# An FFN down projection whose Winograd sums are made earlier and kept in memory

## The chip, the cores and the metric

The kernel runs on one core of a Trainium2 chip. The core has a matmul engine (TensorE, PE in the profile, with its weight loads as PEld), three engines for elementwise work (VectorE or DVE, ScalarE or ACT, GpSimd or POOL), a queue engine that issues all transfers (SyncE or SP), 16 DMA engines, an on-chip memory of 128 partitions (SBUF) and accumulation banks of 128 x 512 float32 (PSUM). The metric is the device time of one execution in microseconds; lower is better. Before the change it is 1144.55 us, the median of three runs (1143.79 to 1145.27).

## What is computed

Two sequences of 512 tokens go through one encoder block, each with 16 shared meta tokens in front: norm, input projection, a gated depthwise convolution beside multi-head latent attention, output projection with residual, and a gated feed-forward network. Only the last part is touched:

```python
hf = _rms(h, ffn_norm_g[i])
h = h + (jax.nn.silu(hf @ w_gate[i]) * (hf @ w_up[i])) @ w_down[i]
...
return _rms(h, final_norm_g)[:, N_META:]
```

h has 1024 tokens by 1024 features, the hidden width D_FF is 2816, that is 22 blocks of 128. All is float32, and must come out at float32 accuracy.

## The kernel before

**Three matmuls for one.** PE multiplies in fp32r, a format with fewer mantissa bits. Each operand is split: ACT copies the rounded high part (L1094 in the down stage, L964 in gate and up), DVE or POOL subtracts it from the value to give the low part (L1096, L966). `mm3` (L151) then issues high·high, high·low and low·high (L158) into the same PSUM bank.

**Winograd's form of Strassen.** All three FFN products are done as 2 x 2 blocks with seven products instead of eight. With blocks a11, a12, a21, a22 of the left side and b11 to b22 of the right, the sums are s1 = a21 + a22, s2 = s1 − a11, s3 = a11 − a21, s4 = a12 − s2 and t1 = b12 − b11, t2 = b22 − t1, t3 = b22 − b12, t4 = b21 − t2 (t4 with that sign in this kernel).

**Gate and up.** 22 units, a gate unit and an up unit for each of the eleven pairs of hidden blocks. A unit has seven products of 12 matmuls of 128x512. While it runs, `comb` makes the operands of the next unit: DVE the sums (L948), ACT the high parts, POOL the low parts. `result` evacuates: DVE adds partial results, ACT applies silu in gate units, DVE multiplies in up units (L1000). The four blocks g of a pair (128 hidden features by 512 tokens each) are stored to memory in `g_dram` (L1001), 256 KB a store. The tiles that hold them (named slots and h) serve the next pair again.

**Down.** The first twenty hidden blocks make ten pairs, taken in three chunks of 3, 3 and 4 pairs. For a chunk, each of the seven products accumulates over the chunk's pairs in four banks: 12 matmuls of 128x512 for a product and a pair, a step. A pair's g and w_down blocks are loaded (L1074), `combine` makes their sums on DVE, in five operations of up to 128x1024 (L1080 to L1084), and `operands` makes the high and low parts for each product (L1094, L1096), the low part on DVE or, two times in seven, on POOL. After each chunk, every product's four banks are added into totals in SBUF (L1207 on ACT for some of the first chunk, L1209 on DVE); after the last chunk the totals are combined (L1178). The last two hidden blocks are multiplied in the ordinary way, eight products or 96 matmuls (operands named re), and with their results go the residual, the final norm and the output, tile by tile (L1231 to L1239).

**What sets the order.** The program text is not the order. A scheduler places each instruction on its engine's queue when it expects its inputs and buffers to be ready; on the chip each queue then runs strictly in that order, waiting where an input is late. SP too works in order: a store that waits for its data holds up the loads behind it.

Of the kernel before, what the change touches and what calls it, by code (L numbers as in the profile page):

```python
# [12 lines left out]
F32 = mybir.dt.float32  # L13
# [5 lines left out]
P = 128  # L19
D = 1024  # L20
# [53 lines left out]
LAST = 2  # L74
CHUNKS = (3, 3, 4)
DOWN_AHEAD = 3
DOWN_MOD = 7
DOWN_POOL = (1, 4)
LOAD_LEAD = (9, 10, 9)
FIRST_AT = {0: ((0, 0),), 1: ((0, 1), (1, 0)), 2: ((0, 2),), 3: ((0, 3), (1, 1),), 4: ((1, 2), (1, 3)), 5: ((2, 0), (2, 1)), 6: ((2, 2), (2, 3))}  # L80
POOL_SUMS = ()
LAST_AT = (1, 2, 3, 4)
LOAD_AT = 5
WO_AT = (4, 6)
FIN_POOL = 0
# [22 lines left out]
def encoder_kernel(ctx: ExitStack, tc: tile.TileContext, x, meta, gains, w_in, w_kr, small, conv_w, wq, wk, wv,  # L108
# [666 lines left out]
    g_dram = [dram.tile([P, NT], F32, name=f"g_dram{f}") for f in range(NFF)]  # L775
# [154 lines left out]
    class Unit:  # L930
# [61 lines left out]
        def result(self, s, e, bk, other, cs):  # L992
            sil = half(4 * s, e)[:, cs]
            if not self.up:
                nc.vector.tensor_add(sil, bk, parts[other][:, cs])
# [4 lines left out]
            nc.vector.tensor_mul(y, y, sil)  # L1000
            nc.sync.dma_start(g_dram[2 * self.p + e][:, s * SEQ:(s + 1) * SEQ], y)  # L1001

    units = [Unit(u) for u in range(NFF)]

# [40 lines left out]

    n_pairs = (NFF - LAST) // 2
    chunks = [list(range(sum(CHUNKS[:i]), sum(CHUNKS[:i + 1]))) for i in range(len(CHUNKS))]
    assert sum(CHUNKS) == n_pairs

    def flat(t):  # L1050
        return t.rearrange("p a b -> p (a b)")

    sets = [("act00_", ops), ("a12", comb), ("s2", comb), ("act01_", ops), ("s1", comb), ("act11_", ops)]

    def reuse(n, pool, x_):
        return flat(pool.tile([P, 4, SEQ], F32R, tag=f"{n}{x_}", bufs=1, name=name("re")))

    class Pair:

        def __init__(self, p):  # L1060
            self.p = p

        def load(self, part):
            if part == 0:
                self.x, self.y = (reuse(*sets[self.p % len(sets)], x_).bitcast(F32) for x_ in "hl")
            g0, g1 = g_dram[2 * self.p], g_dram[2 * self.p + 1]
            w0, w1 = w_down[2 * self.p], w_down[2 * self.p + 1]
            x_, y = self.x, self.y
            lo, hi = slice(0, 512), slice(512, 1024)
            for to, src in (((x_[:, 1024:1536], g0[:, lo]), (x_[:, 512:1024], w0[:, lo])),  # L1070
                            ((y[:, 1024:1536], g1[:, lo]), (y[:, 1536:], w1[:, lo])),
                            ((x_[:, 0:512], g0[:, hi]), (x_[:, 1536:], w0[:, hi]),
                             (y[:, 0:512], g1[:, hi]), (y[:, 512:1024], w1[:, hi])))[part]:
                nc.sync.dma_start(to, src)  # L1074

        def combine(self):

            x_, y = self.x, self.y
            tmp = self.tmp = stream.tile([P, 1024], F32, tag="raw", bufs=2, name=name("raw"))
            nc.vector.tensor_sub(x_[:, 0:1024], x_[:, 1024:], x_[:, 0:1024])  # L1080
            nc.vector.tensor_sub(tmp, y[:, 0:1024], x_[:, 0:1024])  # L1081
            nc.vector.tensor_add(x_[:, 1024:1536], x_[:, 1024:1536], tmp[:, 0:512])
            nc.vector.tensor_sub(x_[:, 1536:], y[:, 512:1024], x_[:, 1536:])
            nc.vector.tensor_sub(y[:, 1024:], y[:, 1024:], tmp)  # L1084

        def operands(self, j, n):

            def of(t, *at):
                return t.rearrange("p (k n) -> p k n", n=512)[:, at[0]:at[-1] + 1:at[-1] - at[0]]

            src = (of(self.x, 1, 2), of(self.y, 2, 3), of(self.tmp, 0, 1) if j == 2 else None, of(self.x, 0, 3),
                   of(self.x, 1, 2), of(self.y, 0, 3), of(self.y, 1, 2))[j]
            w = stream.tile([P, 2, 1024], F32R, tag="pair", bufs=4, name=name("wd"))
            nc.scalar.copy(w[:, :, 0:512], src)  # L1094
            eng = nc.gpsimd if n % DOWN_MOD in DOWN_POOL else nc.vector
            eng.tensor_sub(w[:, :, 512:], src, w[:, :, 0:512].bitcast(F32))  # L1096
            g = 1 if j in (0, 4, 6) else 0
            return w[:, g, :], w[:, 1 - g, :]

    pairs = [Pair(p) for p in range(n_pairs)]  # L1100
    steps = [(c, j, p) for c in range(len(chunks)) for j in range(7) for p in chunks[c]]
    made = {}

    loads = {}
    for n, (c, j, p) in enumerate(steps):
        if c and j < 2:
            free = steps.index((next(c for c in range(len(chunks)) if p - len(sets) in chunks[c]), 6, p - len(sets))) \
                if p >= len(sets) else 0
            for part in ((0,), (1, 2))[j]:
                loads.setdefault(max(n - LOAD_LEAD[part], free, 0), []).append((part, p))  # L1110

    def prepare(upto):
        while len(made) <= min(upto, len(steps) - 1):
            n = len(made)
            c, j, p = steps[n]
            made[n] = pairs[p].operands(j, n)
            at = chunks[c].index(p)
            if j == 1 and at < 2 or j == 2 and at + 2 < len(chunks[c]):
                pairs[chunks[c][at if j == 1 else at + 2]].combine()
            for part, p in loads.pop(n, ()):  # L1120
                pairs[p].load(part)


    def sum_tiles():
        s4_ = [reuse("s4", comb, x_).bitcast(F32) for x_ in "hl"]
        one = lambda t: [t[:, i * 1024:(i + 1) * 1024] for i in range(2)]
        return [hf2, [hres[2], hres[6]], one(s4_[0]), [hres[0], hres[4]], one(s4_[1]), [hres[1], hres[5]],
                [hres[3], hres[7]]]

    def load_h(j, s, e):  # L1130
        for t in range(4):
            nc.sync.dma_start(total[j][t // 2][:, t % 2 * 512:(t % 2 + 1) * 512],
                              h_dram[(4 * s + t) * 128:(4 * s + t + 1) * 128, e * 512:(e + 1) * 512])

    for u in units:
        nxt = units[u.u + 1] if u.u + 1 < NFF else None
        if u.u + 2 < NFF:
            units[u.u + 2].load()
        for j in range(7):
            u.product(j, slice(256, 512) if u.u == 0 else slice(0, 512))  # L1140
            if nxt:
                nxt.comb(j)
                continue
            for part, i in FIRST_AT.get(j, ()):
                if i < CHUNKS[0]:
                    pairs[i].load(part)
            if j >= 6 - DOWN_AHEAD:
                prepare(j - (6 - DOWN_AHEAD))
    total = sum_tiles()
    load_h(1, 0, 0)  # L1150
    load_h(3, 1, 1)
    load_h(5, 1, 0)
    load_h(6, 0, 1)
    for i in range(2):
        nc.gpsimd.tensor_sub(total[5][i], total[5][i], total[3][i])
    g_fin = gain(2)

    last_ops = []

    def load_last():  # L1160
        f = NFF - LAST + len(last_ops)
        if f >= NFF:
            return
        cells = [reuse(*sets[(n_pairs + len(last_ops)) % len(sets)], x_) for x_ in "hl"]
        res = []
        for cell, src in zip(cells, (g_dram[f], w_down[f])):
            raw = stream.tile([P, 1024], F32, tag="raw", bufs=2, name=name("raw"))
            nc.sync.dma_start(raw, src)
            hi, lo = cell[:, 0:1024], cell[:, 1024:]
            nc.scalar.copy(hi, raw)  # L1170
            for a in (slice(0, 512), slice(512, 1024)):
                nc.gpsimd.tensor_sub(lo[:, a], raw[:, a], hi[:, a].bitcast(F32))
            res.append((hi, lo))
        last_ops.append(res)

    def add_total(n, to, other, i):
        eng = nc.gpsimd if n in POOL_SUMS else nc.vector
        eng.tensor_add(total[to][i], total[to][i], total[other][i])  # L1178


    after = {1: ((0, 1, 0),), 2: ((1, 2, 0),), 3: ((2, 3, 2),), 4: ((3, 2, 4), (4, 4, 3)), 5: ((5, 5, 3),),
             6: ((6, 6, 2),)}

    for n, (c, j, p) in enumerate(steps):
        if p == chunks[c][0]:
            if (c * 7 + j) % 2:
                wide = [bank2() for _ in range(2)]
                outs = [wide[t // 2][:, t % 2, :] for t in range(4)]
            else:
                wide = None  # L1190
                outs = [bank() for _ in range(4)]
# [126 lines left out]
```

## Time and profile before

| | us |
|---|---|
| median of the runs | 1144.55 |
| profiled execution, device time | 1145.55 |
| its span, first to last instruction | 1143.8 |
| before the first product of gate and up in full width | 0 to 499 |
| gate and up | to 896.3 |
| down | 896.3 to the end |

The profile is of one execution. A row of a stage table gives its window, then for each engine the busy time and the instructions, then the granted clock of PE (1.00 is full speed), the share of time that the DMA engines were busy, and GB/s. A row of a group gives line, engine, operation, tiles written and read, shape, count, then busy time and mean ns of one, then the idle time of the engine right before these instructions and what ended it. A row in order of time gives start, duration, engine, line and what it was; in brackets the idle time ahead of it. A DMA row gives count, size and the median time from issue to landing. Matmuls overlap, so that the duration of one is longer than the distance to the next.

### The profile page before, as it was taken

How to read it: one execution, taken by the hardware profiler on the slowest of the kernel's cores; microseconds unless marked ns; L12 is line 12 of the kernel's file. 1: busy time of each engine (PE TensorE's matmuls, PEld its weight loads, DVE VectorE, ACT ScalarE, POOL GpSimd, SP SyncE). 2: the span in 40 equal slices, each digit the busy share in tenths (PEclk: the TensorE clock that was granted, in tenths of full speed). 3: DMA queues.
4: the chain of work that ended last, by engine and by line, in shares of the span. 5: the costliest groups of instructions: out<-in, count | busy, mean ns of one | idle time of the engine just before them, and what ended most of it. 6: DMA issues, size and time to landing. Idle time of an engine off the chain costs nothing.

```text
span 1143.8 us, 15672 instructions
## 1 busy us (share of the span) xinstructions
PE 1085.1 (95%) x5886; PEld 933.0 (82%) x5886; DVE 852.5 (75%) x1132; ACT 506.9 (44%) x858; POOL 555.8 (49%) x439
## 2 busy tenths in 40 slices
PE   4999998999989999899999999999999899899896
PEld 4999887888878999788888888888888688687775
DVE  5699997888887547995656565656563877979997
ACT  6455525787785535633322332232223344233425
POOL 6489735563562323584554455445543442223815
PEclk9999999999999999899999999999999999999899
DMA  8211111110111312322232223222313974110203
GB/s 279 78 38 39 45 41 55 37 56 1 38 38 59 127 38 93 136 86 77 90 93 73 77 89 94 73 77 89 95 53 112 357 258 138 37 37 1 74 1 147
DMA packets 38554, 98.01 MB, mean 86 GB/s; under 512 B 4544, under 2 KB 4800, under 8 KB 38480
## 3 DMA queue, kind: packets, MB, share of 16 engines
q1 hardware_dynamic: 38480, 97.02, 25.4%
q8 instruction: 46, 0.75, 0.3%
q14 instruction: 28, 0.23, 0.1%
HBM read 77.08 MB, written 19.92 MB: 85 GB/s over the span
## 4 chain that ended last, share of the span: by engine, by line
PE 64%; DVE 26%; POOL 3%; issue 3%; ACT 2%; DMA 2%; SPq 0%; POOLq 0%; DVEq 0%; ACTq 0%
PE pt L158 50%; PE ps L158 7%; DVE wd L1096 3%; DVE ps L336 3%; DVE ps L344 3%; PE pt L652 2%; PE pt L622 2%; DVE pacc L346 1%; POOL wd L1096 1%; DMA re<-in_w_down_dram 1%; DVE re L1178 1%; DVE raw L1081 1%; DVE slots L1209 1%; DVE hf L881 1%; DVE y L1237 1%
## 5 line engine op out<-in xcount | busy, mean ns | idle before, releaser
L158 PE MATMUL pt<-act_h,wc 128*128 128x512 f32 (+1 forms) x552 | 176.2, 382 | 0.1
L966 POOL TENSOR_TENSOR wc<-tt,wc 128x512 fp32r<-128x512 f32 x84 | 112.9, 1361 | 110.1 <-ACT wc L964 62.2
L158 PE MATMUL pt<-hn_h,wp 128*128 128x256 f32 (+2 forms) x576 | 131.9, 322 | 1.1 <-ACT hn_h L148 1.1
L158 PEld LDWEIGHTS pt<-act_h,wc 128*128 128x128 f32 x552 | 103.3, 190 | 19.9 <-issue 0.3
L158 PE MATMUL pt<-wd 128*128 128x512 f32 x444 | 107.1, 395 | 5.8 <-DVE wd L1096 4.8
L158 PE MATMUL ps<-wd 128*128 128x512 f32 x396 | 99.5, 407 | 10.0 <-POOL wd L1096 5.4
L158 PE MATMUL pt<-act_l,wc 128*128 128x512 f32 (+1 forms) x276 | 105.6, 383 | 3.5 <-DVE act_l L900 3.4
L964 ACT CAST wc<-tt 128x512 fp32r<-128x512 f32 x88 | 51.2, 617 | 122.8 <-PE pt L158 119.5
L158 PEld LDWEIGHTS pt<-wd 128*128 128x128 f32 x444 | 83.9, 190 | 25.9 <-DVE wd L1096 6.6
L158 PEld LDWEIGHTS pt<-hn_h,wp 128*128 128x128 f32 x576 | 96.5, 190 | 10.1 <-ACT hn_h L148 1.5
L158 PEld LDWEIGHTS ps<-wd 128*128 128x128 f32 x396 | 78.0, 198 | 28.8 <-POOL wd L1096 5.9
L1094 ACT CAST wd<-re 128x1024 fp32r<-128x1024 f32 x60 | 62.9, 1053 | 86.5 <-PE pt L158 36.1
L144 POOL TENSOR_TENSOR wp<-raw,wp 128x1024 fp32r<-128x1024 f32 x28 | 69.2, 2471 | 54.4 <-ACT wp L141 54.3
L1096 POOL TENSOR_TENSOR wd<-re,wd 128x1024 fp32r<-128x1024 f32 x16 | 49.8, 3114 | 93.6 <-ACT wd L1094 79.8
L158 PE MATMUL pt<-hn_l,wp 128*128 128x256 f32 (+2 forms) x288 | 93.2, 324 | 0.0
L1096 DVE TENSOR_TENSOR wd<-re,wd 128x1024 fp32r<-128x1024 f32 x44 | 65.3, 1493 | 21.0 <-ACT wd L1094 21.0
L597 POOL TENSOR_SCALAR p<-p,sst 128x512 f32<-128x512 f32 x64 | 44.1, 694 | 67.5 <-DVE sst L595 59.4
L158 PE MATMUL pt<-wp,act_h 128*128 128x256 f32 x384 | 71.4, 285 | 1.6 <-DVE h L844 1.5
L966 POOL TENSOR_TENSOR wc<-raw,wc 128x512 fp32r<-128x512 f32 x30 | 39.3, 1323 | 54.0 <-ACT wc L964 54.0
L158 PEld LDWEIGHTS pt<-act_l,wc 128*128 128x128 f32 x276 | 52.4, 190 | 13.6 <-DVE act_l L900 3.6
L158 PEld LDWEIGHTS pt<-wp,act_h 128*128 128x128 f32 x384 | 60.1, 192 | 2.0 <-DVE h L844 1.7
L314 POOL TENSOR_TENSOR pacc<-pacc,prod 128x512 f32<-128x512 f32 x43 | 58.3, 1356 | 7.0 <-ACT prod L312 4.3
(294 smaller groups left out, 2870.3 us busy)
## 6 DMA issues: line engine op xcount, KB each, us to landing
raw<-in_w_gate_dram SPq DMA_DIRECT2D x22, 512.0 KB, 3.8
g_dram<-slots SPq DMA_DIRECT2D x44, 256.0 KB, 2.2
re<-g_dram SPq DMA_DIRECT2D x40, 256.0 KB, 5.3
re<-in_w_down_dram SPq DMA_DIRECT2D x40, 256.0 KB, 5.3
raw<-in_w_in_dram SPq DMA_DIRECT2D x12, 512.0 KB, 3.7
slots<-in_w_up_dram SPq DMA_DIRECT2D x11, 512.0 KB, 3.5
h<-in_w_up_dram SPq DMA_DIRECT2D x11, 512.0 KB, 3.5
x<-in_x_dram SPq DMA_DIRECT2D x8, 512.0 KB, 4.8
```

Source lines behind the costliest of these rows:

```text
L144: nc.gpsimd.tensor_sub(lo[:, a], raw[:, a], hi[:, a].bitcast(F32))
L158: nc.tensor.matmul(out_ap, lhsT=w_, rhs=m_, start=first and i + j == 0, stop=last and i == n - 1 and j == 2)
L314: nc.gpsimd.tensor_add(acc, acc, to)
L336: nc.vector.scalar_tensor_tensor(a_, half_win(c, 0, i, HS + 1), k, a_, ALU.mult, ALU.add)
L344: nc.vector.scalar_tensor_tensor(m_, both[:, :, i:i + HS], k, m_, ALU.mult, ALU.add)
L597: nc.gpsimd.tensor_scalar(pr[:, real], pr[:, real], st[:, 2, t:t + 1], 1.0, op0=ALU.mult, op1=ALU.mult)
L622: nc.tensor.transpose(pt[:, t * 128:(t + 1) * 128], self.ps[t][:, n0:n0 + w], ident)
L652: nc.tensor.matmul(self.po, lhsT=v, rhs=p_, start=self.done + j == 1, stop=self.done + j == 5)
L964: nc.scalar.copy(w[:, 0:512], src)
L966: lo_eng.tensor_sub(w[:, 512:1024], src, w[:, 0:512].bitcast(F32))
L1094: nc.scalar.copy(w[:, :, 0:512], src)
L1096: eng.tensor_sub(w[:, :, 512:], src, w[:, :, 0:512].bitcast(F32))
```

## The change

The sums of the down product are no longer made in the down stage. Those of g (four DVE operations of 128x512 for a pair, `g_sums`) are made in the up unit, right after the results, and stored with g: a11 with s1, a12 with a22, s3 with s2, and s4, which makes 1.8 MB for a pair where it was 1 MB. Those of w_down (`w_sums`) are made in the gate and up units as well, in halves of 256 columns, two groups for a pair: load two blocks' halves into the one buffer of the tag "gain" (tile wt), four DVE operations of 128x256, two stores. The down stage then has 77 steps, seven products of eleven pairs, without chunks and without the two blocks done in the ordinary way. Each step loads its two blocks of 128x512 (`load_step`, two transfers of 256 KB, issued 12 steps ahead in the text, into places that hold eight steps) and makes its operands (`prepare`, high on ACT, low on DVE, never on POOL; 14 places). A product takes all eleven pairs in one accumulation of four banks; the next product uses four others. The results go straight to where they belong (`evacuate`): into hres, which is loaded again with the residual, and into the four tiles x_. The last product is taken a token tile at a time, and the final norm of tiles 4 to 6 follows each; of the last tile, the half that is ready is squared and scaled by the gain ahead.

```diff
-LAST = 2
-CHUNKS = (3, 3, 4)
-DOWN_AHEAD = 3
-DOWN_MOD = 7
-DOWN_POOL = (1, 4)
...
+DOWN_AHEAD = 4
+LOAD_AHEAD = 8
+ORDER_DOWN = (0, 1, 2, 4, 3, 6, 5)
...
             nc.vector.tensor_mul(y, y, sil)
-            nc.sync.dma_start(g_dram[2 * self.p + e][:, s * SEQ:(s + 1) * SEQ], y)
...
+    def g_sums(p, j):
+        a11, a21, a12, a22 = half(3, 0), half(3, 1), half(7, 0), half(7, 1)
+        s3_, s2_, s4_ = hf2[0][:, 0:512], hf2[0][:, 512:], hf2[1][:, 0:512]
+        if j == 5:
+            nc.vector.tensor_sub(s3_, a11, a21)
+            nc.vector.tensor_add(a21, a21, a22)
+            nc.sync.dma_start(d_a11s1[p], hres[3])
+        elif j == 6:
+            nc.sync.dma_start(d_a12a22[p], hres[7])
+            nc.vector.tensor_sub(s2_, a21, a11)
+            nc.sync.dma_start(d_s3s2[p], hf2[0])
+        elif j == 7:
+            nc.vector.tensor_sub(s4_, a12, s2_)
+            nc.sync.dma_start(d_s4[p], s4_)
...
+    def w_sums(p, r, j):
+        cs = slice(r * 256, (r + 1) * 256)
+        def cut(t):
+            return t.rearrange("p (i c) -> p i c", i=2)[:, :, cs]
+        if j == 0:
+            w_tile[0] = const.tile([P, 4, 256], F32, tag="gain", bufs=1, name=name("wt"))
+            for i in range(2):
+                nc.sync.dma_start(w_tile[0][:, 2 * i:2 * i + 2], cut(w_down[2 * p + i]))
+        w = w_tile[0]
+        b11, b12, b21, b22 = (w[:, i] for i in range(4))
+        if j == 3:
+            nc.vector.tensor_sub(b11, b12, b11)
+        elif j == 4:
+            nc.vector.tensor_sub(b12, b22, b12)
+            nc.sync.dma_start(cut(d_t1t3[p]), w[:, 0:2])
+        elif j == 5:
+            nc.vector.tensor_sub(b22, b22, b11)
+        elif j == 6:
+            nc.vector.tensor_sub(b21, b21, b22)
+            nc.sync.dma_start(cut(d_t4t2[p]), w[:, 2:4])
...
+    steps = [(j, p) for j in ORDER_DOWN for p in range(n_pairs)]
...
+    ld_places = ["act00_h", "act00_l", "a12h", "a12l"]
+    op_places = [None] * 4 + [n + x_ for n in ("s2", "act01_", "s1", "act11_", "s4") for x_ in "hl"]
...
+            nc.sync.dma_start(t[:, 0, :], a)
+            nc.sync.dma_start(t[:, 1, :], b)
...
+            nc.scalar.copy(w[:, :, LO], blocks[n])
+            nc.vector.tensor_sub(w[:, :, HI], blocks[n], w[:, :, LO].bitcast(F32))
...
             u.product(j, slice(256, 512) if u.u == 0 else slice(0, 512))
+            if u.up:
+                g_sums(u.p, j)
+                w_sums(u.p, 0, j)
+            elif u.p:
+                if j == 0:
+                    g_sums(u.p - 1, 7)
+                w_sums(u.p - 1, 1, j)
...
+    def evacuate(j, t, src):
+        if j == 0:
+            nc.scalar.copy(x_[t], src)
+            add_sum(t, 0, src)
+        elif j == 1:
+            add_sum(t, 0, src)
+        elif j == 2:
+            nc.vector.tensor_add(x_[t], src, x_[t])
+        elif j == 4:
+            add_sum(t, 1, src)
+            add_sum(4 + t, 1, src)
+        elif j == 3:
+            add_sum(t, 1, x_[t])
+            nc.vector.tensor_add(x_[t], src, x_[t])
+        elif j == 6:
+            add_sum(t, 1, src)
+            for e in range(2):
+                add_sum(4 + t, e, x_[t])
...
+    for n, (j, p) in enumerate(steps):
+        load_step(n + DOWN_AHEAD + LOAD_AHEAD)
+        prepare(n + DOWN_AHEAD + (n_pairs if n >= 5 * n_pairs else 0))
...
+            step_mm(n, t, sums[t], p == 0, p == n_pairs - 1)
+            if p == n_pairs - 1:
+                evacuate(j, t, sums[t])
```

Where the scheduler put the new work shows in three places. The first is SP's queue in the middle of gate and up, a pair's worth: before, with the loads of the next units and four stores of g,

```order
L1001 DMA g_dram8_3992<-slots_67 128x512
L1001 DMA g_dram9_3993<-slots_67 128x512
L1001 DMA g_dram8_3992<-slots_67 128x512
L1001 DMA g_dram9_3993<-slots_67 128x512
L940 DMA raw_984_6799<-in_w_gate_dram 128x1024
```

and after, with w sums of pairs 8 and 9 (wt is the tile of a group, d_t1t3 and d_t4t2 the memory blocks, here with the pair's number behind):

```order
L1031 DMA wt_1127_8116<-in_w_down_dram 128x2x256 x2
L1038 DMA d_t1t38_4036<-wt_1127_8116 256x1x256
L1043 DMA d_t4t28_4047<-wt_1127_8116 256x1x256
L938 DMA slots_67<-in_w_up_dram 128x1024
L1031 DMA wt_1142_8255<-in_w_down_dram 128x2x256 x2
L1038 DMA d_t1t39_4037<-wt_1142_8255 256x1x256
L938 DMA raw_992_6940<-in_w_gate_dram 128x1024
L1043 DMA d_t4t29_4048<-wt_1142_8255 256x1x256
```

The load of a group stands right behind the stores of the group before it, which read the same buffer, and a weight load stands between. The text has one group for a unit; the queue has two, and the last of the 22 groups stands in unit 12.

The second is DVE where the last token tile is made into FFN operands and the first gate unit runs (act_l, s2l and the like are low parts that PE waits for; L907 to L912 here are L909 to L914 before). Before there was no wt row among these:

```order
L898 TENSOR_TENSOR a12l_4708<-slots_67,a12h_4707 128x4x128
L1035 TENSOR_TENSOR wt_845_5654<-wt_845_5654 128x256
L903 TENSOR_TENSOR slots_67<-slots_67,px_827_5475 128x512
L1037 TENSOR_TENSOR wt_845_5654<-wt_845_5654 128x256
L898 TENSOR_TENSOR act11_l_4058<-slots_67,act11_h_4057 128x4x128
L906 TENSOR_TENSOR slots_67<-slots_67 128x512
L1040 TENSOR_TENSOR wt_845_5654<-wt_845_5654 128x256
L912 TENSOR_TENSOR act01_l_4056<-slots_67,act01_h_4055 128x4x128
L907 TENSOR_TENSOR slots_67<-slots_67,px_827_5475 128x512
L909 TENSOR_TENSOR slots_67<-slots_67 128x512
L1042 TENSOR_TENSOR wt_845_5654<-wt_845_5654 128x256
L912 TENSOR_TENSOR s2l_4712<-slots_67,s2h_4711 128x4x128
```

Four w sums of the first group now stand among them, ahead of s2l.

The third is DVE at the end of the last unit, where the operands of the first down steps (L1130; wd_1184 and wd_1186 are those of steps 2 and 3, the re tiles those of steps 4 to 9) alternate with the unit's results (L983 to L998):

```order
L983 TENSOR_TENSOR slots_67<-pt_1179_8591,h1_4063 128x512
L997 TENSOR_TENSOR slots_67<-pt_1179_8591,slots_67 128x512
L1130 TENSOR_TENSOR re_1201_8748<-re_1189_8681,re_1201_8748 128x2x512
L1130 TENSOR_TENSOR wd_1184_8637<-re_1183_8634,wd_1184_8637 128x2x512
L998 TENSOR_TENSOR slots_67<-slots_67 128x512
L1130 TENSOR_TENSOR re_1204_8783<-re_1190_8686,re_1204_8783 128x2x512
L997 TENSOR_TENSOR slots_67<-pt_1182_8615,slots_67 128x512
L1130 TENSOR_TENSOR re_1202_8765<-re_1189_8681,re_1202_8765 128x2x512
L1130 TENSOR_TENSOR re_1205_8800<-re_1190_8686,re_1205_8800 128x2x512
L997 TENSOR_TENSOR slots_67<-pt_1185_8640,slots_67 128x512
L998 TENSOR_TENSOR slots_67<-slots_67 128x512
L1130 TENSOR_TENSOR wd_1186_8662<-re_1183_8634,wd_1186_8662 128x2x512
```

Step 3's operand comes after those of steps 4 to 9; PE's queue has the first three steps in front of it, in the same order as its text.

More of the change, by code (lines that the diff above doesn't have):

```diff
@@ L1043, in encoder_kernel @@
     units[1].load()
[L1046 to L1110, printed above, removed]
+    n_pairs = NFF // 2
@@ L1143, in encoder_kernel @@
                 continue
[L1144 to L1155, printed above, removed]
-    g_fin = gain(2)
[L1158 to L1174, printed above, removed]
```

171 lines of the change are left out of this document (91 added, 80 removed).

## The prediction

> **What bounds the kernel now.** I read the page's busy times first, then busy time by stage, then PE's groups and PE in order of time in the last stage, and last the chain of waits there.
>
> ```profile
> span 1143.8 us, 15672 instructions
> PE 1085.1 (95%) x5886; PEld 933.0 (82%) x5886; DVE 852.5 (75%) x1132; ACT 506.9 (44%) x858; POOL 555.8 (49%) x439
> ```
>
> PE is busy 95%, but an average says little. By stage (columns: PE, PE's weight loads, DVE, ACT, POOL, granted clock, DMA share, GB/s):
>
> ```profile
> 480.00:500.00 20.00, 16.14 (x98) 14.81 (x99) 19.83 (x23) 9.88 (x20) 15.92 (x12) 0.84 0.27 83
> 500.00:880.00 380.00, 380.00 (x1678) 314.66 (x1677) 222.67 (x259) 112.48 (x200) 189.36 (x142) 1.00 0.26 82
> 880.00:896.00 16.00, 16.00 (x72) 13.26 (x71) 9.26 (x9) 3.49 (x4) 2.39 (x1) 1.00 0.90 301
> 896.30:1134.90 238.60, 222.81 (x937) 179.69 (x935) 212.39 (x194) 93.46 (x117) 94.75 (x42) 0.96 0.30 106
> ```
>
> From 500 to 896 (gate and up products) PE never stops, and DVE is busy 59%. From 896.3 to 1134.9 (down products) PE loses time, DVE is busy 89%, and the clock falls to 0.96. At 480 to 500, where gate products begin, DVE is full.
>
> ```profile
> L158 PE MATMUL pt<-wd 128*128 128x512 f32 x444 | 107.1, 395 | 5.8 <-DVE wd L1096 4.8 <-DVE hf L1209 0.7 <-ACT wd L1094 0.2
> L158 PE MATMUL ps<-wd 128*128 128x512 f32 x396 | 99.5, 407 | 10.0 <-POOL wd L1096 5.4 <-DVE wd L1096 3.8 <-ACT wd L1094 0.5
> L158 PE MATMUL pt<-re,re 128*128 128x512 f32 x96 | 21.9, 389 | 0.0
> ...
> 896.33 6.28 PE L158 MATMUL pt<-wd 128*128 128x512 f32 x27
> 902.45 0.61 PE L158 MATMUL ps<-wd 128*128 128x512 f32 x2
> ...
> 914.25 7.87 PE L158 MATMUL ps<-wd 128*128 128x512 f32 x22 [5.43 <-POOL wd L1096]
> 921.95 5.60 PE L158 MATMUL pt<-wd 128*128 128x512 f32 x24
> ...
> 1070.94 5.49 PE L158 MATMUL ps<-wd 128*128 128x512 f32 x12 [3.12 <-DVE wd L1096]
> ...
> 1112.96 21.92 PE L158 MATMUL pt<-re,re 128*128 128x512 f32 x96
> ```
>
> The down stage has 444 + 396 + 96 = 936 matmuls. Unhindered, 27 take 902.45 − 896.33 = 6.12 us, 0.2267 us each, so 936 need 212.2. The last ends at 1112.96 + 21.92 = 1134.9, 238.6 after the first: 26.4 too many. 15.8 of them are the waits in the groups' last column; the other 10.6 are slow matmuls right behind the waits (22 in 921.95 − 914.25 = 7.70 us, 0.35 each, where 0.2267 is the pace).
>
> **The rule and the row.** The Trainium skill, page "TensorE: Matmul & The Clock Gate", Part 1, says that PE's clock falls to half after an idle window of some 3.4 us and comes back after as long a busy one. By it only the 5.43 us wait costs anything behind itself. The trace disagrees: behind a wait of 3.12 us, a row of 12 matmuls still shows 5.49 us, about 0.45 each. I go by the trace, where a microsecond of waiting costs 26.4 / 15.8 = 1.67; by the rule the stalls of 3 us that I put in the sum below would stay 2.
>
> What PE waits for is always a finished operand (wd), and the chain of waits shows why one is late:
>
> ```profile
> 904.97 9.23 POOL L1096 TENSOR_TENSOR wd<-re,wd 128x1024 fp32r<-128x1024 f32 x1 [10.17 <-ACT wd L1094]
> ...
> 1064.21 2.23 DVE h L1178
> 1066.45 2.23 DVE slots L1178
> 1068.68 2.21 DVE wd L1096
> ```
>
> Either POOL's subtraction takes 9.23 us beside a busy DVE, or DVE does Winograd sums (L1080 to L1084), additions into the totals (L1209, L1178) and operands in turn, and the operand is last.
>
> **The change, part by part.** *Matmuls.* 77 steps of 12 make 924 in place of 936: 924 × 0.2267 = 209.5 us.
>
> *DVE in the down stage.* The sums of ten pairs go, and so does POOL's share of the operands. Left are 77 operands, 44 additions of 128x512 (per tile, seven products ask for 1, 1, 1, 2, 2, 3 and 1 of them) and the norms.
>
> ```profile
> L1096 DVE TENSOR_TENSOR wd<-re,wd x44: 1208/1218/3419, 885.7 to 1108.2; 128x1024 fp32r<-128x1024 f32 x44
> ...
> L1209 DVE TENSOR_TENSOR slots<-slots,pt 128x512 f32<-128x512 f32 x14 | 8.9, 678 | 1.1 <-PE pt L158 1.1
> ...
> L1094 ACT CAST wd<-re 128x1024 fp32r<-128x1024 f32 x58 | 60.8, 1053 | 77.1 <-PE pt L158 36.1 <-PE ps L158 34.8 <-DMA re<-in_w_down_dram 2.9
> ```
>
> 77 × 1.22 + 44 × 0.68 = 124 us, plus some 10 for the norms: 134 of 210, where 212 of 239 were busy. A step lasts PE 12 × 0.2267 = 2.72; its operand costs ACT 1.05 and DVE 1.22. Neither can hold PE up on the average, and no long DVE job is left to stand before an operand. Since an evacuation comes once in eleven steps into banks that the next product does not use, a wait for it goes too. I take all 26.4 us as removed inside the stage; the lower bound is that none is.
>
> *DMA in the down stage.* Each step loads 512 KB, so 524 KB / 2.72 us = 193 GB/s; 880 to 896 shows 301 GB/s carried. Loads are issued eight or more steps (21 us) ahead. Hidden.
>
> *The seam.* The order shows PE going from the last gate/up product to steps 0 to 2, whose operands ACT and DVE make while the last unit's results are still being evacuated, in buffers that its products free one by one. From the fourth product of that unit on (896.3 − 3 × 2.72 = 888.1) DVE has, by the order, 8 operands and 7 result operations up to step 3's operand: 8 × 1.22 + 7 × 0.68 = 14.5, so that is done near 903. PE has steps 0 to 2, 36 × 0.2267 = 8.2 us, and asks for it at 904.5. The margin of 2 us holds if every load is there in time. Best case no wait; worst, the 5.43 of today comes back, 9 with its slow matmuls. I take 3.
>
> *Added to gate and up.* Per pair, DVE gets four g sums of 128x512 and eight w sums of 128x256, and SP gets w loads and stores beside larger g stores. The order has the w sums of all pairs early: 22 groups, two in each unit, so within the first eleven of 22 units.
>
> ```profile
> L1000 DVE TENSOR_TENSOR slots<-slots 128x512 f32<-128x512 f32 x22 | 23.1, 1048 | 0.4
> L995 DVE TENSOR_TENSOR slots<-pt,slots 128x256 f32<-128x256 f32 x2 | 0.8, 420 | 0.1
> ...
> L948 DVE TENSOR_TENSOR tt<-raw,tt 128x512 f32<-128x512 f32 x20 | 34.8, 1742 | 25.0 <-POOL wc L966 25.0
> ...
> g_dram<-slots SPq DMA_DIRECT2D x40, 256.0 KB, 2.2
> ...
> h<-h_dram SPq DMA_DIRECT2D x2, 256.0 KB, 2.8
> ...
> re<-in_w_down_dram SPq DMA_DIRECT2D x40, 256.0 KB, 5.3
> ```
>
> Two units last 168 × 0.2267 = 38.1 us. DVE's 59% is 22.3 of them; 4 × 1.05 and 16 × 0.42 make 33.2. If each w sum also meets POOL as L1000 does (1.05 instead of 0.68), it is 39, just over. Behind a late DVE wait PE's results, and PE has three other banks: 3 × 12 × 0.2267 = 8.2 us of cover, gone only if the lateness adds up.
>
> It could add up, because the groups use one tile (wt) in turn: stores of one must land before the next is loaded, and DVE, which works in order, stands at the first sum until the load is there. A link: store 2.2, load 2.8, a second issue and two hand-overs about 0.4, so 5.4; its sums and what stands between them about 3. Four links in 38.1 us: 4 × 8.4 = 33.6. Hidden, with 4.5 to spare. Below: nothing. Above: a load of 5.3, as in the crowded down stage, makes a link of 10.9.
>
> At the stage's start, the order puts four w sums into the full 480 to 500 stretch, ahead of the operand s2l: 4 × 0.42 = 1.7, up to 7 if each meets POOL. I take 2 there and 2 for the rest: 4.
>
> *The end.* The last result then goes through one addition, half a square, the root and the scaling:
>
> ```profile
> 1135.27 0.68 DVE L1231 TENSOR_TENSOR slots<-pt,slots 128x512 f32<-128x512 f32 x1
> 1135.98 0.63 ACT L1232 ACTIVATE y<-slots 128x512 f32<-128x512 f32 x1 [1.08 <-DVE slots L1231]
> ...
> 1138.04 0.53 DVE L1233 SCALAR_TENSOR_TENSOR rs<-ms,ms 128x1 f32<-128x1 f32 x1 [0.61 <-ACT y L1232]
> 1138.64 0.55 POOL L1234 TENSOR_TENSOR rs<-rs,tiny 128x1 f32<-128x1 f32 x1
> ...
> 1139.23 0.75 DVE L1237 SCALAR_TENSOR_TENSOR y<-re,rs,gain 128x512 f32<-128x512 f32 x1 [0.66 <-POOL rs L1234]
> ```
>
> Now 1143.8 − 1134.9 = 8.9. Without the second half in between: 0.4 to the addition, 0.7, 0.8, 0.6, 0.6, 0.8, then 3.8 from 1139.98 to the end: 7.7.
>
> **Sum.** 896.3 + 4 + 209.5 + 3 + 7.7 = 1120.5 against 1143.8. That profiled run took 1145.55, 1.75 beside its span and 1.0 above the median of 1144.55; so 0.75 is added: **1121 us**, 2% less. This case's own range is 1113 (none of the two delays; 1114.3) to 1128.
>
> **Rivals.**
> *The seam stalls.* 9 us idle at the start of the stage, 15 with slow matmuls, for 3: 1133. For it: that is where today's longest wait stands. Against: no POOL, no sums there.
> *DVE is full in the first half of gate and up.* The Trainium skill, page "SBUF — State Buffer", "Who interferes with whom", has DVE and POOL share a port pair under an exclusive lock. The rows show it as L948's 1.74 us beside POOL. As a mechanism here: 16 w sums a pair at 0.42 + 1.0 make 22.3 + 4.2 + 22.7 = 49.2, but only about every other one meets POOL (busy 189 of 380): 41.2, 3.1 over, 5.5 times, 17 less the 8.2 of cover: 9, with slow clock 15: 1133.
> *The wt chain sets the pace: slower.* At links of 10.9, 43.6 per pair, 5.5 over, 5.5 times: 30, less 8.2: 22 idle, 22 to 37 lost where I put 2: 1141 to 1156, and I put it at 1150, the more as these stores and loads go in rows of 1 KB where the quoted ones have 2 KB or more. It costs from links of 9.5 on and turns the change slower at links between 10.6 (slow matmuls counted) and 11.1. For it: one buffer, in-order DVE and SP. Against: DMA share is 0.26 there, and a 256 KB load lands in 2.8.
> *The stalls stay.* If cast and subtraction alone made operands late, 26.4 return in place of 3: 1144. Against: 1.05 and 1.22 in 2.72.
>
> **Chances.** Forecast 0.69, seam 0.10, port 0.08, chain 0.09, stalls stay 0.04. Two tenths of a per cent (2.3 us) is about what a measurement can tell from none. Faster: 0.69 + 0.10 + 0.08 = 0.87; the same 0.04; slower 0.09. The range takes in the seam and port cases: 1113 to 1138.
>
> **What would show it.** PE's groups of the down stage: 924 matmuls, idle under 3 us, clock 1.00; the first of them between 896 and 901. DVE in that stage near 134. PE idle from 500 to 700 would speak for the chain (DVE then waits at L1035 for a DMA) or the port (DVE busy over 95%). Waits at steps 2 or 3 would speak for the seam. Wrong in the large: PE waiting for wd or re all through the stage, or for a load.

## The result, and the profile after

The changed kernel takes 1152.42 us, median of five runs (1150.46 to 1156.38). The kernel before, on the same chip, takes 1143.79. The ratio is 1.0081, with a 95% interval of 1.0058 to 1.0105: 0.8% slower, where I forecast 2% faster. The profiled execution is the slowest of the five, 1156.38 us. First the page, then busy time by stage (the columns are those of the prediction's table).

```profile
span 1154.6 us, 15888 instructions
PE 1089.3 (94%) x5874; PEld 935.1 (81%) x5874; DVE 837.4 (73%) x1197; ACT 499.0 (43%) x832; POOL 471.5 (41%) x409
```

```profile
480.00:500.00 20.00, 14.27 (x94) 13.24 (x95) 19.62 (x26) 10.77 (x21) 13.19 (x8) 0.83 0.41 132
500.00:720.00 220.00, 195.41 (x802) 155.97 (x801) 158.72 (x225) 52.68 (x96) 96.50 (x71) 0.95 0.54 175
720.00:937.90 217.90, 217.90 (x964) 180.46 (x963) 148.40 (x177) 69.90 (x118) 102.30 (x74) 1.00 0.40 133
937.90:1147.50 209.60, 209.60 (x925) 173.29 (x923) 125.88 (x131) 81.84 (x88) 8.70 (x14) 1.00 0.60 207
```

The down stage is what was hoped for: 209.6 us, PE never idle, clock 1.00. Before it took 238.6. But gate and up, which never stopped PE before, now lose 24.6 us of PE's time between 500 and 720, and the clock falls to 0.95 there. The two profiled executions' own times differ by 1156.38 − 1145.55 = 10.8 us, and three differences make that up:

| | before | after | difference |
|---|---|---|---|
| end of gate and up | 896.3 | 937.9 | +41.6 |
| down products | 238.6 | 209.6 | −29.0 |
| from the last matmul to the end | 8.9 | 7.1 | −1.8 |

In the view of waits, over the time from 478 on for PE and from 500 to 760 for DVE (columns: us in total, times, longest), the reason shows at once.

```profile
PE pt L151 <- DVE slots L997: 16.7, 9, 2.9
PE pt L151 <- DVE h L979: 6.7, 5, 2.7
```

```profile
DVE wt L1035 <- DMA wt<-in_w_down_dram: 44.0, 16, 6.0
...
DVE wt L1037 <- DMA wt<-in_w_down_dram: 4.3, 5, 1.4
```

PE waits for DVE to take its results out of the banks (L997, L979). DVE is not too busy for that (158.72 of 220 us): it stands at the first w sum of a group, L1035, for 44 us, because w_down's piece has not landed. In order of time, SP's and DVE's rows, a link of the chain through the one buffer wt looks like this.

```profile
565.44 0.56 SPq L1043 DMA_DIRECT2D d_t4t<-wt  x1
567.98 1.25 SPq L1031 DMA_DIRECT2D wt<-in_w_down_dram  x2
573.31 0.56 SPq L1038 DMA_DIRECT2D d_t1t<-wt  x1
575.78 0.56 SPq L1043 DMA_DIRECT2D d_t4t<-wt  x1
```

```profile
571.01 0.73 DVE L1035 TENSOR_TENSOR wt<-wt 128x256 f32<-128x256 f32 x1 [3.80 <-DMA wt<-in_w_down_dram]
571.67 0.68 DVE L983 TENSOR_TENSOR slots<-pt,h 128x512 f32<-128x512 f32 x1
572.27 0.67 DVE L997 TENSOR_TENSOR slots<-pt,slots 128x512 f32<-128x512 f32 x1
...
575.34 0.41 DVE L1042 TENSOR_TENSOR wt<-wt 128x256 f32<-128x256 f32 x1
```

At 565.44 the second store of a group is issued. It lands, and only then, at 567.98, can the loads into the same buffer go out; at 571.01 the first of the two loads has landed, which is all that the first sum reads, and DVE, which has stood still for 3.80 us, starts the four sums. Results that PE had ready meanwhile (L983, L997) come in between. The next second store goes out at 575.78: 10.3 us for this link. PE stands for 2.22 us behind that L997:

```profile
573.09 0.47 PE L151 MATMUL pt<-a12h,wc 128*128 128x512 f32 x1 [2.22 <-DVE slots L997]
```

The first and the last of 21 such stores between 500 and 740 are these.

```profile
508.18 0.56 SPq L1043 DMA_DIRECT2D d_t4t<-wt  x1
...
733.82 0.56 SPq L1043 DMA_DIRECT2D d_t4t<-wt  x1
```

(733.82 − 508.18) / 20 = 11.28 us a link. The rows between give the mean of its three parts: 3.10 from the store's issue to the load's, 3.47 from there to the first sum, 4.71 from the first sum to the next second store. A unit of gate and up lasts 19.04 us, and the order has two groups in each: 22.56 − 19.04 = 3.5 us too long, in ten or eleven units 35 to 39 us. What PE lost from 500 to 720 is 38.8: it did 802 matmuls there, and at full pace 973 (the row of before, quoted with the second experiment, has just that), so 171 × 0.2267. After 733.8, when the last group is done, PE never waits again.

### The profile page after: what moved, and what is told of

Same layout as the page of the kernel before. It is cut to its first block, busy times and chain, and to the rows that moved or that the text cites. A ratio compares the mean times of both kernels' runs of the same rounds, so it can differ in the third digit from the quotient of the medians.

```text
span 1154.6 us, 15888 instructions
## 1 busy us (share of the span) xinstructions
PE 1089.3 (94%) x5874; PEld 935.1 (81%) x5874; DVE 837.4 (73%) x1197; ACT 499.0 (43%) x832; POOL 471.5 (41%) x409
## 4 chain that ended last, share of the span: by engine, by line
PE 59%; DVE 21%; DMA 12%; issue 3%; ACT 2%; POOL 1%; SPq 1%; DVEq 0%; POOLq 0%; ACTq 0%
PE pt L151 41%; PE ps L151 12%; DMA wt<-in_w_down_dram 5%; DMA d_t4t<-wt 5%; DVE ps L329 3%; DVE ps L337 3%; PE pt L645 2%; PE pt L615 2%; DVE pacc L339 1%; DVE wt L1037 1%; DVE wt L1035 1%; DVE tt L946 1%; DVE wt L1042 1%; DVE hf L879 1%; DMA raw<-in_w_in_dram 1%
## 5 line engine op out<-in xcount | busy, mean ns | idle before, releaser
L176 POOL TENSOR_SCALAR ms<-ms 128x1 f32<-128x1 f32 (+1 forms) x24 | 12.8, 534 | 250.5 <-ACT re L175 213.8
L1130 DVE TENSOR_TENSOR re<-re,re 128x1024 fp32r<-128x1024 f32 x53 | 64.2, 1223 | 47.2 <-ACT re L1129 46.8
L1129 ACT CAST re<-re 128x1024 fp32r<-128x1024 f32 x53 | 55.2, 1054 | 68.0 <-PE ps L151 23.8
L151 PE MATMUL pt<-re 128*128 128x512 f32 x360 | 84.0, 389 | 0.0
L151 PEld LDWEIGHTS pt<-re 128*128 128x128 f32 x360 | 67.6, 188 | 14.0
L964 POOL TENSOR_TENSOR wc<-raw,wc 128x512 fp32r<-128x512 f32 x30 | 42.1, 1419 | 79.8 <-ACT wc L962 79.8
L151 PE MATMUL pt<-a12h,wc 128*128 128x512 f32 (+1 forms) x184 | 63.7, 411 | 10.7 <-DVE slots L997 10.6
L151 PE MATMUL pt<-s4h,wc 128*128 128x512 f32 (+1 forms) x184 | 60.1, 390 | 6.7 <-DVE h L979 6.7
L151 PE MATMUL ps<-re 128*128 128x512 f32 x276 | 63.9, 389 | 0.0
```

Of the source, the lines that this page charges most:

```text
L151: nc.tensor.matmul(out_ap, lhsT=w_, rhs=m_, start=first and i + j == 0, stop=last and i == n - 1 and j == 2)
L176: nc.gpsimd.tensor_scalar(ms[:rows], ms[:rows], EPS, 0.0, op0=ALU.add, op1=ALU.add)
L964: lo_eng.tensor_sub(w[:, 512:1024], src, w[:, 0:512].bitcast(F32))
L1129: nc.scalar.copy(w[:, :, LO], blocks[n])
L1130: nc.vector.tensor_sub(w[:, :, HI], blocks[n], w[:, :, LO].bitcast(F32))
```

## The experiments

Three theories. A: the chain of store, load and sums through one buffer sets the pace of gate and up. B: DVE is too full, with POOL beside it. C: something else that the change added, the g sums or the larger stores. In all kernels that are made from the changed one, the sums are queued on DVE behind a fixed earlier instruction, so that their place is known. Their first w sum is L1042, the last L1052, the load L1037 and the second store L1053, but for the kernel whose loads go elsewhere (L1049 first).

**One group in each unit.** `behind()` queues a sum behind the DVE instruction that the program issued last, here the result of the product j (in an up unit, behind products 5 and 6, the g sum that follows it).

```diff
-            nc.vector.tensor_sub(b11, b12, b11)
+            with behind():
+                nc.vector.tensor_sub(b11, b12, b11)
...
             if u.up:
                 g_sums(u.p, j)
-                w_sums(u.p, 0, j)
-            elif u.p:
-                if j == 0:
-                    g_sums(u.p - 1, 7)
-                w_sums(u.p - 1, 1, j)
+            elif u.p and j == 0:
+                g_sums(u.p - 1, 7)
+            w_sums(u.p, u.up, j)
```

> The changed kernel with each group of w sums queued behind the products of its own gate or up unit: one group per unit over 22 units in place of two in units 0 to 12. Nothing is left out. Theory A (the chain through the one wt buffer set the pace): a link of 11.3 us fits into the 19.04 us of a unit, DVE stops waiting at the first sum (now 44 us), gate and up end at 897 to 903 in place of 937.9, and the time is 1152.4 - 41.6 + (1 to 6): 1112 to 1117. Theory B (DVE itself is too full with the 176 sums of 128x256, slowed by POOL): spread over 22 units the sums cost less at a time, so a part comes back, 1115 to 1135, with DVE over 90% busy in places. Theory C (it is the g sums and the larger stores of g, which are not moved): 1145 to 1155.

Measured: 1138.62 us, ratio to before 0.9955 (0.9934 to 0.9976); its ten runs spread more than those of the other kernels, from 1134.13 to 1145.47. The median lies in no theory's range. DVE still waits:

```profile
DVE wt L1042 <- DMA wt<-in_w_down_dram: 59.7, 11, 7.5
```

```profile
505.26 0.56 SPq L1053 DMA_DIRECT2D d_t4t<-wt  x1
...
906.44 0.57 SPq L1053 DMA_DIRECT2D d_t4t<-wt  x1
```

Here the first and the last of 21 second stores are (906.44 − 505.26) / 20 = 20.06 us apart, longer than a unit. My arithmetic had taken over the link of 11.3, but a link contains its sums, and I had put these behind four products in turn: they took 11.24 us of it. The rest grew too, from 6.6 to 8.8, of which 1.4 lies between the store's issue and the load's (4.48 where it was 3.10): SP has the unit's own stores and loads between the two. So a turn of the buffer was again longer than a unit, and gate and up again went at the pace of the chain, 22 × 1.0 = 22 us too slow; they end at 918.56, 22.2 us later than in the kernel before. Here the seam cost something as well. The loads of the down stage come late, ACT and DVE stand for them, PE waits for a result of the last unit, and the down stage takes 5.8 us longer than in the changed kernel:

```profile
923.47 6.70 PE L151 MATMUL pt<-wd 128*128 128x512 f32 x21 [3.85 <-DVE slots L997]
```

It made a new question, whether the sums in the turn or SP's queue held up the units, to which the kernel with its sums together comes back below.

**Two groups in each unit, with the chain and without it.** Two kernels, alike in the number of sums, stores and transfers. The first is the changed kernel with known places (of the two groups of a unit, the first has its sums behind products 1 and 2, the second behind 5 and 6); in the second, the loads after the first group go to a piece of SBUF that nothing reads, queued behind the store whose landing they waited for before, and the sums work on what is in wt. So w_down's sums are not those of the reference there. Since the sums still overwrite what the stores read, DVE still waits for stores, 12.1 us from 500 to 760.

```diff
+            if 1 <= u.u <= n_pairs:
+                for r in range(2):
+                    for k in TWO[r][j]:
+                        w_sums(u.u - 1, r, k)
```

```diff
-                nc.sync.dma_start(w_tile[0][:, 2 * i:2 * i + 2], cut(w_down[2 * p + i]))
+                to = w_tile[0][:, 2 * i:2 * i + 2] if first else spare
...
+                    nc.sync.dma_start(to, cut(w_down[2 * p + i]))
```

> The changed kernel with the w sums written at fixed places: two groups in each of units 1 to 11, the first behind products 1 and 2, the second behind products 5 and 6. Nothing is left out. It is the counterpart of the next run, and should behave as the changed kernel does. Theory A (chain): two links of 11.3 us in a unit of 19.04 us, so 3.5 us lost a unit in 11 units, 39 in all: 1145 to 1156, and DVE waits over 30 us for loads of wt. Theory B (DVE too full): 1140 to 1155, with DVE over 90% busy between 520 and 740. Theory C (g sums): 1145 to 1155.

> As the run with two groups a unit, and with as many loads, stores and sums, but after the first group the loads go to a spare piece of SBUF that nothing reads, and the sums work on what lies in wt: DVE's work, the stores and the transfers are all there, only the wait of the sums for a load is gone (w_down's sums are then not those of the reference). Theory A (chain): DVE never stands for a load, 1112 to 1122, gate and up end before 905. Theory B (DVE too full with POOL beside it): nothing changes against the run with two groups, 1140 to 1155. Theory C (g sums and larger stores, or the transfers' crowd): nothing changes either.

Measured: 1154.54 us (ratio 1.0093, 1.0070 to 1.0116) with the chain, 1117.38 us (0.9764, 0.9746 to 0.9783) without. DVE's wait with the chain, from 500 to 750, and then the rows of 500 to 720 of three kernels, before, with the chain, without:

```profile
DVE wt L1042 <- DMA wt<-in_w_down_dram: 57.5, 15, 5.3
```

```profile
500.00:720.00 220.00, 220.00 (x973) 182.16 (x972) 132.35 (x153) 64.42 (x115) 111.80 (x84) 1.00 0.28 87
```

```profile
500.00:720.00 220.00, 199.83 (x835) 160.65 (x834) 163.68 (x221) 53.70 (x96) 99.59 (x71) 0.96 0.52 175
```

```profile
500.00:720.00 220.00, 220.00 (x973) 182.14 (x972) 204.14 (x265) 63.65 (x114) 120.01 (x83) 1.00 0.63 205
```

This decides between the theories. Without the wait for loads, DVE is busy 204 of 220 us, with POOL busy 120, and PE does its 973 matmuls without a stop. So neither a full DVE (B) nor the g sums and the traffic (C, here 205 GB/s) cost PE anything; 37 us hang on the sums' wait for the load. It wasn't that SP had less to wait for either. Each load into the spare piece waits for the one before it, and from 500 to 750 SP stands longer in front of these loads (L1044) than it does with the chain, where it is 42.9 us:

```profile
SPq L1044 <- DMA hf<-in_w_down_dram: 76.7, 33, 5.2
```

**Half as many bytes in a link.** Groups of 128 columns; the other half of w_down's sums is left out.

```diff
-        cs = slice(r * 256, (r + 1) * 256)
+        cs = slice(r * 128, (r + 1) * 128)
```

> As the run with two groups a unit, but each group has half the columns (128 in place of 256; the other half of w_down's sums is left out, and the down stage loads as many bytes from w_down itself). Theory A with a link made of bytes: store, load and sums shrink by a third or more, the link falls from 11.7 to below 9.5, two fit into a unit, and the time is 1116 to 1124. Theory A with a link made of fixed times (issue, landing, hand-overs, waits in DVE's queue): it stays at 10.5 to 11.5, 1 to 2 us too long, eleven times two: 1135 to 1152. Theory B (DVE too full): DVE's w sums take 0.27 in place of 0.42 to 0.88 us each, 1120 to 1140.

Measured: 1130.42 us (0.9882, 0.9857 to 0.9906), between the two ranges of theory A (and in that of B, which the pair above had ruled out). The rows of transfers from 500 to 750, with full and with half groups (count, size, median us to landing), and DVE's wait with half groups:

```profile
wt<-in_w_down_dram SPq DMA_DIRECT2D x42, 256.0 KB, 3.2
d_t1t<-wt SPq DMA_DIRECT2D x21, 256.0 KB, 2.5
```

```profile
wt<-in_w_down_dram SPq DMA_DIRECT2D x42, 128.0 KB, 2.6
d_t1t<-wt SPq DMA_DIRECT2D x22, 128.0 KB, 2.2
```

```profile
DVE wt L1042 <- DMA wt<-in_w_down_dram: 43.1, 15, 6.1
```

Half the bytes, in rows half as long, take 0.6 us off a load and 0.3 off a first store (0.4 off a second). The first and the last of 22 second stores, with full groups and with half groups:

```profile
511.37 0.55 SPq L1053 DMA_DIRECT2D d_t4t<-wt  x1
...
760.24 0.87 SPq L1053 DMA_DIRECT2D d_t4t<-wt  x1
```

```profile
511.38 0.57 SPq L1053 DMA_DIRECT2D d_t4t<-wt  x1
...
736.53 0.65 SPq L1053 DMA_DIRECT2D d_t4t<-wt  x1
```

The mean link went from 248.87 / 21 = 11.85 to 225.15 / 21 = 10.72 us, and two of these still don't fit into 19.04. Nearly all of the difference is in the sums' part, 4.86 to 3.75; the store's part shrank from 3.07 to 2.71, and that from the load's issue to the first sum grew, from 3.92 to 4.25. Most of a link is not bytes. A line through both sizes, an estimate, leaves 2.0 us for a load and 1.9 for a store of nothing. The Trainium skill, page "DMA: Bandwidth & Descriptors", section "Anatomy of one DMA", splits a transfer's time into a fixed part of about 2.0 us and one that goes with the bytes; the page's figure is for another way of issuing, but the fixed part of these rows agrees with it.

**No store in the link.** The same with full groups, whose sums are not stored; the down stage reads w_down itself in their place.

```diff
-            nc.sync.dma_start(cut(d_t1t3[p]), w[:, 0:2])
...
-            nc.sync.dma_start(cut(d_t4t2[p]), w[:, 2:4])
```

> As the run with two groups a unit, full width, but the w sums are not stored (the down stage loads as many bytes from w_down itself, so its products are not the reference's). In that run a link was 3.1 us for the store, 3.8 from the load's issue to the first sum and 4.8 for the sums and what stands between them. Theory A (chain): without the store the link is 3.8 + 4.8 = 8.6 us, under the 9.5 that two links in a unit leave: DVE's wait for loads of wt falls from 57 us to under 15, gate and up end before 906, 1115 to 1124. Theory A2 (the load alone is what holds DVE; the store is hidden beside other work): over 30 us of waits stay, 1135 to 1150. Theory B (DVE too full): 1140 to 1155.

Measured: 1118.01 us (0.9776, 0.9756 to 0.9795), as theory A has it. The rest of DVE's wait is 15.0 us at L1042 and 1.3 at the second sum, a little over the 15 expected:

```profile
DVE wt L1042 <- DMA wt<-in_w_down_dram: 15.0, 10, 3.7
```

```profile
500.00:720.00 220.00, 219.95 (x971) 181.90 (x970) 199.54 (x261) 62.88 (x113) 122.06 (x83) 1.00 0.46 149
```

These waits cost PE nothing: of 973 matmuls it misses 2. A link cut from two different sides, at the load or at the store, gives the same time within 0.6 us.

**One group in each unit, its sums together.** Nothing is left out; this is a whole kernel. The load is issued at product 0, all four sums stand behind product 2. The edit is shown against the first experiment.

```diff
+    ONE = ((0,), (), (3, 4, 5, 6), (), (), (), ())
...
-            w_sums(u.p, u.up, j)
+            for k in ONE[j]:
+                w_sums(u.p, u.up, k)
```

> As the run with one group a unit, but all four w sums of a group stand together behind product 2 of the unit, and not behind products 3 to 6. Nothing is left out. Theory A (chain): in that run the sums took 11.2 us of the link, since they waited for four products in turn, and the link was 20.06 us, longer than the unit's 19.04. Together they take about 4, so the link can be 3.1 + 3.8 + 4.5 = 11.4, 7.6 us shorter than a unit: DVE does not stand for wt, gate and up end at 897 to 902, and the time is 1115 to 1121. Theory S (it is SP: stores that wait for a sum hold up the unit's own loads behind them): the order of SP's queue is the same kind as there, 1130 to 1140 again. Theory B (DVE too full): no change against that run, 1135 to 1140.

Measured: 1117.97 us (0.9773, 0.9758 to 0.9788), 2.3% faster than the kernel before and 3.0% faster than the changed one. DVE waits 2.5 us in all for loads of wt, PE goes through gate and up with 0.56 us lost from 500 on, and the down products follow at 900.52:

```profile
DVE wt L1042 <- DMA wt<-in_w_down_dram: 1.4, 1, 1.4
DVE wt L1045 <- DMA wt<-in_w_down_dram: 1.1, 1, 1.1
```

```profile
500.00:900.00 400.00, 399.44 (x1762) 330.89 (x1763) 312.52 (x404) 123.32 (x214) 204.69 (x143) 1.00 0.50 169
```

```profile
900.52:1110.10 209.58, 209.58 (x925) 173.29 (x923) 126.30 (x131) 82.11 (x89) 8.71 (x14) 1.00 0.61 211
```

That also answers most of the question left by the first experiment. The sums now take 4.74 us of a turn, where they took 11.24, and 2.69 lie between the store's issue and the load's, where it was 4.48; what is left of a unit is slack before the first sum. The unit's own loads were not late in the first experiment either: from 500 to 905 neither DVE nor ACT nor POOL once waited for a gate or up weight. So it was the turn of the buffer, and most of what was saved in it are the sums. But only 1.0 us had to be saved, and whether the 1.8 at SP alone would have done it was not tried.

**What made the old down stage stall.** The kernel before with POOL's share of the operands on DVE, and, the other way round, the best kernel with two low parts in seven on POOL.

```diff
-DOWN_POOL = (1, 4)
+DOWN_POOL = ()
```

```diff
-            nc.vector.tensor_sub(w[:, :, HI], blocks[n], w[:, :, LO].bitcast(F32))
+            lo_eng = nc.gpsimd if n % 7 in (1, 4) and n > 4 else nc.vector
+            lo_eng.tensor_sub(w[:, :, HI], blocks[n], w[:, :, LO].bitcast(F32))
```

> The kernel before the change with all low parts of the down stage on DVE, none on POOL (20 operations of 128x1024 moved). Nothing is left out. Theory P (the stalls of the old down stage come from POOL's long operation): its 10.0 us behind POOL go, with their slow matmuls 1.67 times as much, 1128 to 1136. Theory D (they come from DVE's sums standing ahead of operands): DVE gets 20 x 1.22 = 24 us more, 236.8 of 238.6, so operands come later still: 1146 to 1165.

> As the run with one group a unit and its sums together, and in the down stage the low part of two steps in seven on POOL, as the kernel before had it. Nothing is left out. Theory P (POOL's operation is late whenever DVE works beside it): with DVE busy 57% instead of 89%, POOL's 2.5 us become 4 or more and stalls return, 5 to 12 us over the run without POOL. Theory D (POOL's operation was late only because Winograd sums kept DVE busy without a gap): 0 to 2 us over the run without POOL.

Measured: the first takes 1129.70 us (0.9876, 0.9853 to 0.9900), within theory P; the second 1118.32 us (0.9774, 0.9758 to 0.9790), the same as without POOL, within theory D. In the groups of the down stage (to 1118), rows of the kernel before and of the kernel before without POOL's share, and then POOL's line in the best kernel with POOL's share (shortest, median and longest in ns):

```profile
L1096 DVE TENSOR_TENSOR wd<-re,wd 128x1024 fp32r<-128x1024 f32 x43 | 64.1, 1499 | 19.6 <-ACT wd L1094 19.6
L1081 DVE TENSOR_TENSOR raw<-re,re 128x1024 f32<-128x1024 f32 x10 | 18.5, 1854 | 0.1
...
L1096 POOL TENSOR_TENSOR wd<-re,wd 128x1024 fp32r<-128x1024 f32 x15 | 47.4, 3162 | 79.3 <-ACT wd L1094 65.5 <-DMA re<-in_w_down_dram 8.1 <-DVE slots L1209 5.7
```

```profile
L1096 DVE TENSOR_TENSOR wd<-re,wd 128x1024 fp32r<-128x1024 f32 x58 | 74.5, 1301 | 12.0 <-ACT wd L1094 11.9
...
L1081 DVE TENSOR_TENSOR raw<-re,re 128x1024 f32<-128x1024 f32 x10 | 12.2, 1219 | 0.0
```

```profile
L1141 POOL TENSOR_TENSOR re<-re,re x15: 2394/2402/3367, 899.1 to 1068.4; 128x1024 fp32r<-128x1024 f32 x15
...
L1141 POOL TENSOR_TENSOR wd<-re,wd x5: 2392/2692/3371, 914.2 to 1060.3; 128x1024 fp32r<-128x1024 f32 x5
```

And the down stage by its busy times, of the kernel before without POOL's share and of the best kernel with it:

```profile
898.10:1118.10 220.00, 214.67 (x937) 174.75 (x935) 206.04 (x211) 93.08 (x117) 41.40 (x23) 1.00 0.32 112
```

```profile
900.00:1117.00 217.00, 210.19 (x925) 172.89 (x923) 118.92 (x115) 83.03 (x93) 63.10 (x36) 0.99 0.60 206
```

Taking POOL away brings 14.1 us of the old kernel's time by a change of one line, but not the whole 26: PE still stands for 5.3 of the 220 us, behind operands that DVE (2.7) and ACT (2.6) finish late. So the old stage has stalls without POOL too. DVE takes over 20 operations of 1.22 us and yet is busy for 206.0 us where it was 212.4, since its other operations get shorter (1854 to 1219 ns, 1499 to 1301). The new stage, which has no sums, brings all 26, and there POOL's operation does no harm: DVE is busy 118.92 of 217 us, and the operation takes 2.4 us, never more than 3.4. The one of 9.23 us came only where POOL worked beside a DVE that was busy 89%. The new stage has lost more than the sums (the chunks and the additions into totals), so which of these makes POOL harmless is not shown.

## Why the prediction was wrong

**Where the step failed.** It is the sum's term "2 there and 2 for the rest: 4" for what is added to gate and up, which measured 41.6, and in it the link: "5.4; its sums and what stands between them about 3", 8.4, "hidden, with 4.5 to spare". It measured 11.28. Each part came out longer: the store 3.10 where I had 2.2 and a hand-over; the loads 3.47 where I had 2.8 and an issue; and the sums 4.71 where I had 3, because results and weight sums stand between them, and beside POOL they take longer (884 ns for the mean first sum; of all 84 sums in these links, the 34 that overlap an operation of POOL take 1.07 us on average, the other 50 take 0.43):

```profile
L1035 DVE TENSOR_TENSOR wt<-wt 128x256 f32<-128x256 f32 x21 | 18.6, 884 | 52.3 <-DMA wt<-in_w_down_dram 44.0 <-issue 8.3
```

The last is 1.7 of the 2.9 us that were missing. I had the right mechanism, its place and its tipping point: the rival "the wt chain sets the pace", which costs from links of 9.5 on and turns the change slower between 10.6 and 11.1, at 1150 us. It got a chance of 0.09. What I held against it, the DMA engines' share of 0.26 and a load that lands in 2.8, was no argument: a link that is mostly latency and waiting in turn doesn't need busy engines. And a forecast of 8.4 against a limit of 9.5, made from four durations each of which can grow in company, deserved to be taken for an even chance.

**The other terms, on the changed kernel's trace.**
- Matmuls in the down stage: 209.5 forecast, 209.6 measured.
- "I take all 26.4 us as removed inside the stage": right, clock 1.00 and no wait.
- DVE there: 134 forecast, 125.88 measured.
- The transfers of the down stage, 193 GB/s by the sum and 207 measured: hidden, as forecast; PE waits for none.
- Seam: 3 forecast, none measured, but closely: step 3's operand is done at 945.36, and PE gets to it 36 matmuls after 937.89, at 946.05. Of the margin of 2 us 0.7 was left.
- First stretch: 2 forecast. The kernel before with its POOL share moved, whose gate and up are untouched, starts the down products later by itself,

```profile
898.13 2.20 PE L158 MATMUL pt<-wd 128*128 128x512 f32 x9
```

so 1.8 us of the 41.6 are within what two executions of the same instructions differ by. Of the 41.6, 38.8 fall between 500 and 720; with 1.8 of the rest unsure, what the four early sums cost can't be told.
- The end: 7.7 forecast, 7.1 measured.

The best kernel, with the chain out of the way, ends gate and up at 900.5, takes 209.6 for the down products and 7.1 for the end: 1117.2, where the sum had 1120.5. That sum was right for a kernel that the scheduler did not make, and with some luck: of the 4.2 us in gate and up, only 0.56 were lost after 500, and the 3 for the seam cost nothing.

**The rivals.** The seam stalls did not come in the changed kernel, only in the first experiment. The port case was wrong in its price: w sums do get longer beside POOL (1.07 us, where it had 1.42), but DVE at 204 of 220 us held nobody up. Of the old stalls, POOL's share was a cause, as shown above, and not the only one, and I could not have told their shares from the trace of before.

**The rule of the clock.** A microsecond of waiting cost 38.8 / 24.6 = 1.58 between 500 and 720, where none of PE's waits was over 2.9 us. The prediction had 1.67 from the trace of before; by the Trainium skill, page "TensorE: Matmul & The Clock Gate", Part 1, waits below the idle window of some 3.4 us would cost only themselves. The measurement decides: many short waits also bring the granted clock down, here to 0.95.

## What to carry to other kernels

When work is hoisted into a stage with spare engine time, and goes through one buffer as load, compute, store, add up the whole turn (store landing, load landing, every instruction that the order puts between) and compare it with the room between two turns; busy shares of DMA and DVE said nothing of it here. An engine that works in order stops for everybody at the first instruction whose load is late, so a hoisted group must be paced, and its own steps put close together. And look where the scheduler has put the new work, since it places it as early as its inputs seem ready: the text had one group for a unit, the queue two. Of the 34 us between the changed kernel and the best one, one group for a unit, as the text has it, brings back 13.8, and putting the sums together the other 20.7.

## What was not expected of the hardware

Halving a transfer from 256 to 128 KB in rows of 1 KB and 512 bytes took only 0.6 us from a load of 3.2 and 0.3 from a store of 2.5. A DVE that was busy 93% of the time, with POOL working beside it for more than half of it, did not delay PE once in 220 us, while one that was busy 72% and stood still for loads, up to 6.0 us at a time, cost 25 us of PE's time. Whether a second buffer for wt would do as well as pacing was not tried.
